# Hybrid conformer and MLA block: new durations and a longer assumed landing time in the kernel's own scheduler

## Chip, cores, metric

One core of one Trainium2 chip. The metric is the device time of one execution in microseconds; the median of several runs counts. The profile is one more execution, taken by the hardware profiler.

## What is computed

One decoder block on x (512 tokens of width 1024, float32). Six vectors of width 1024 (shift, scale and gate for the mixer and for the MLP) come from the conditioning vector c by one product with w_ada; they modulate the normalised x. Cut to what matters:

```python
mod = silu(c) @ w_ada + b_ada                      # 1024 -> 6 * 1024
shift1, scale1, gate1, shift2, scale2, gate2 = split(mod, 6)
h = rms_norm(x, g_pre_mix) * (1 + scale1) + shift1
u_glu, q_lat, kv_lat, k_r, gate_logits = split(h @ w_in)
u = causal_depthwise_conv(ua * sigmoid(ub), conv_w, conv_b)      # 31 taps, 1024 channels
y_a = silu(layer_norm(u, conv_norm_g, conv_norm_b)) @ w_conv_out
o = mla_attention(q_nope, q_rope, k_nope, k_rope, v)             # 8 heads, causal
y_b = o @ w_attn_out
y = (sigmoid(g_a) * y_a + sigmoid(g_b) * y_b) @ w_out
x = x + gate1 * rms_norm(y, g_post_mix)
h = rms_norm(x, g_pre_mlp) * (1 + scale2) + shift2
x = x + gate2 * rms_norm(square(relu(h @ w_mlp_in)) @ w_mlp_out, g_post_mlp)
```

## The kernel before

Each float32 product is made of three products of a rounded form: an operand is split into a high half (a cast by ScalarE, ACT) and a low half (a subtraction by VectorE, DVE), and `mm3` (line 454) issues high x high, high x low and low x high on TensorE (PE). Weights are loaded by SyncE (SP) in units of 512 KB or so, split, used and dropped (`wunit`, line 492). All buffers lie in two large tiles, `f_arena` (float32) and `r_arena` (the split halves), and in the eight banks of `psum`; an allocator gives out places, and an instruction that writes a place waits until whoever read it before has finished.

**The stages in the order of PE's work:** the first input products, with shift1 and scale1 made just in time (to about 70 us); the rest of the input projection; attention by heads (from about 150 to 275 us): `proj` (line 1008) makes q and k of a head, and `v_pair` (984) makes V for two heads; `scores` (1032) makes four tiles of scores and a softmax; `pv` (1057) transposes the probabilities on PE, splits them into halves and multiplies by V. For the last two heads V is kept in float32 and copied by ACT out of psum. Then the products with w_attn_out, the gates, a LayerNorm, w_conv_out, w_out, and from about 510 us the MLP in four chunks.

**Work beside it.** The depthwise convolution is 31 multiply-adds for each of eight channel tiles, all on DVE with the weights in the tile `cw` (`conv_ops`, line 783; 240 scalar_tensor_tensor and 8 tensor_scalar in all). They depend on nothing but each other and may stand anywhere until the LayerNorm. The modulation rows for gate1, shift2 and scale2 are made in attention by `ada_by_dma` (1134): SP loads 1 MB of w_ada (two blocks of 1024 columns by 128 partitions); ACT multiplies each block by the matching column of c (`act.mul`, operand `cT`); GpSimd (POOL) issues a DMA which adds the block to one of three sums in `f_arena`. That is 12 loads, 24 multiplications and 21 adding transfers. Transfers into the same sum follow one another, each waiting for the last to land. The loaded buffer comes free only when its adding transfers have landed.

**What sets the order.** Nothing runs in the order of the code. Every call goes to `Planner.record` (245), which stores it with its cost (`cost`, 217) and the calls it depends on. `Planner.plan` (306) then plays the program through: at each moment each engine takes, of the calls whose inputs are ready, PE the earliest in the code, and every other engine the one that is due first (a few calls have a bonus); due times are worked back from PE's sequence. A DMA is held to occupy a common channel for its bytes and to land 910 ns after it. The calls are then issued in the order of their starts (line 388, the line of nearly all instructions in the profile). So each engine gets a fixed queue. The whole is repeated up to eight times with buffers placed by the lifetimes of the time before, and the repetition with the shortest plan is kept.

Of the kernel before, what the change touches and what calls it, by code (L numbers as in the profile page):

```python
# [45 lines left out]
PV32 = (3,)  # L46
PASSES = 8
LEAD = 15000.0
ADAS = (1, 1, 0, 4)
KGRP = ((2, 3), (4, 5), (6,), (7,))  # L50
HX, HA, HG, HC = 1.2e5, 1e5, 3e3, 1.1e5
# [109 lines left out]


class Op:
    __slots__ = ("i", "eng", "fn", "a", "k", "cost", "post", "deps", "succ", "dead", "t0", "t1", "ndep", "ready", "dma", "rank", "hurry", "bufs", "raw")


class Planner:
# [6 lines left out]
    def __init__(self, nc, spaces):  # L174
        self.spaces = spaces
        self.real = dict(pe=nc.tensor, act=nc.scalar, dve=nc.vector, pool=nc.gpsimd, sp=nc.sync)
        self.ops = []
        self.last_w = {}
        self.reads = {}
        self.boost = 0  # L180
        self.hurry = 0.0
        self.after = None

    class Engine:
        def __init__(self, plan, name):
# [31 lines left out]
    def cost(self, eng, fn, outs, ins, k):  # L217

        n = max(self.free_size(o) for o in (ins if fn == "reduce_sum" else outs))
        if fn == "dma_start":  # L220
            return 475.0, 2000.0
        psum = any(r.tensor.name.startswith("psum") for r in ins + outs)
        if eng == "pe":
            if fn == "transpose":
                return 0.85 * n + 1, 190.0
            if ins[0].dtype == F32:
                return max(53.5, n / 2.4 + 2) * 4, 190.0
            return max(64.0, n / 2.4 + 2.5), 190.0
        scalars = sum(isinstance(v, bass.AP) and self.free_size(v) == 1 for v in ins) if n > 1 else 0
        if eng == "act":  # L230
            t = 0.833 * n + (51 if psum else 93) + 93 * scalars
            if fn == "activation" and any(isinstance(v, bass.AP) for v in outs[1:]):
                t += 93
            return t, 150.0
        if eng == "dve":
            if fn in ("tensor_copy", "tensor_scalar"):
                return (1.04 if psum else 0.52) * n + 68 + 61 * scalars, 150.0
            if fn == "scalar_tensor_tensor":
                return 1.04 * n + 130, 150.0
            return 1.04 * n + 70, 150.0  # L240
        if fn == "memset":
            return 36.0, 100.0
        return (460.0 if ALU.pow in self.args else 160.0) + 1.0 * n, 150.0

    def record(self, eng, fn, a, k):
        self.args = a
        aps = [v for v in a if isinstance(v, bass.AP)]
        names = dict(k)
        outs, ins = [], []
        if "out" in names:  # L250
            outs.append(names.pop("out"))
        else:
            outs.append(aps.pop(0))
        if fn == "tensor_tensor_reduce":
            outs.append(aps.pop())
        if isinstance(names.get("accum_out"), bass.AP):
            outs.append(names.pop("accum_out"))
        ins = aps + [v for v in names.values() if isinstance(v, bass.AP)]
        o = Op()
        o.i, o.eng, o.fn, o.a, o.k = len(self.ops), eng, fn, a, k  # L260
        o.succ, o.dma, o.rank, o.hurry = [], None, len(self.ops) - self.boost, self.hurry
        o.cost, o.post = self.cost(eng, fn, outs, ins, k)
        if fn == "dma_start":
            b = 4
            for _, c in outs[0].ap:
                b *= c
            o.dma = b
        deps = set()
        rd = [self.region(r) for r in ins]
        wr = [self.region(w) for w in outs]  # L270
        o.bufs = set()
        for nm, units in rd + wr:
            for sp in self.spaces:
                if nm.startswith(sp):
                    o.bufs.add((sp, self.spaces[sp].owner[units[0]]))
        for nm, units in rd:
            lw, rs = self.last_w.setdefault(nm, {}), self.reads.setdefault(nm, {})
            for u in units:
                if u in lw:
                    deps.add(lw[u])  # L280
        o.raw = set(deps)
        for nm, units in wr:
            lw, rs = self.last_w.setdefault(nm, {}), self.reads.setdefault(nm, {})
            for u in units:
                if u in lw:
                    deps.add(lw[u])
                if u in rs:
                    deps.update(rs[u])
        for nm, units in rd:
            rs = self.reads[nm]  # L290
            for u in units:
                rs.setdefault(u, []).append(o.i)
        for nm, units in wr:
            lw, rs = self.last_w[nm], self.reads[nm]
            for u in units:
                lw[u] = o.i
                rs.pop(u, None)
        deps.discard(o.i)
        if self.after is not None:
            deps.add(self.after)  # L300
        o.deps = deps
        for d in deps:
            self.ops[d].succ.append(o.i)
        self.ops.append(o)

    def plan(self):
        ops = self.ops
        pe_t = 0.0
        big = sum(o.cost for o in ops if o.eng == "pe") + TAIL
        for o in ops:  # L310
            o.dead = big
            if o.eng == "pe":
                pe_t += o.cost
                o.dead = pe_t
        for o in reversed(ops):
            lat = o.post + (o.dma / 180.0 if o.dma else 0.0)
            for s in o.succ:
                q = ops[s]
                o.dead = min(o.dead, q.dead - q.cost - lat)
        heaps = {e: [] for e in self.NAMES}  # L320
        free = {e: 0.0 for e in self.NAMES}
        dma_free = 0.0
        future = []

        def key(o):
            return (o.rank, o.i) if o.eng == "pe" else (o.dead - o.hurry, o.i)

        for o in ops:
            o.ndep, o.ready = len(o.deps), 0.0
            if not o.ndep:  # L330
                heapq.heappush(future, (0.0, o.i))
        order = []
        now = 0.0
        while len(order) < len(ops):
            while future and future[0][0] <= now:
                o = ops[heapq.heappop(future)[1]]
                heapq.heappush(heaps[o.eng], (key(o), o.i))
            for e in self.NAMES:
                if free[e] <= now and heaps[e]:
                    o = ops[heapq.heappop(heaps[e])[1]]  # L340
                    o.t0 = now
                    free[e] = now + o.cost
                    if o.dma:
                        st = max(now + 1100.0, dma_free)
                        dma_free = st + o.dma / 360.0
                        o.t1 = dma_free + 910.0
                    else:
                        o.t1 = free[e] + o.post
                    order.append(o)
                    for s in o.succ:  # L350
                        q = ops[s]
                        q.ndep -= 1
                        q.ready = max(q.ready, o.t1 if (q.eng != o.eng or o.dma) else free[e] if e == "pe" else max(free[e], o.t1 - 30))
                        if not q.ndep:
                            heapq.heappush(future, (q.ready, q.i))
            nxt = [free[e] for e in self.NAMES if free[e] > now and heaps[e]]
            if future:
                nxt.append(future[0][0])
            if not nxt:
                break  # L360
            now = max(now, min(nxt)) if min(nxt) > now else now
        assert len(order) == len(ops)
        self.length = max(o.t1 for o in ops)
        return order
# [28 lines left out]
def tile_hybrid_block(  # L393
# [48 lines left out]
    def emit(past, replay):  # L442
# [3 lines left out]
        plan = Planner(nc, dict(f_arena=fa, r_arena=ra, psum=pb))  # L446
        pe, act, dve, pool, sp = (plan.engine(e) for e in Planner.NAMES)
# [52 lines left out]
        st = tile_of([P, 96], F32, "stats")  # L500
# [43 lines left out]
        for t in range(NT):  # L544
            b = fa.alloc(D)
# [7 lines left out]
        for i, vecs in enumerate(((("bada", b_ada), ("gpm", g_pre_mix)),  # L553
# [5 lines left out]
            for nm, src in vecs:  # L559
                n = src.shape[1] // P  # L560
# [50 lines left out]
        for k in range(KD):  # L611
            b = pb.alloc()
# [77 lines left out]
        for ks in KGRP:  # L690
            plan.hurry = HA - 1e4 * ks[0]
            n = len(ks) * P
# [441 lines left out]
        def ada_by_dma(parts):  # L1134
# [3 lines left out]
                ada_acc[part] = fa.alloc(D)  # L1138
            for u in range(4):
                for part in parts:  # L1140
                    acc = fa.v(ada_acc[part])
                    b = fa.alloc(2 * D)
                    v = fa.v(b, "p (j n) -> p j n", j=2)
                    sp.dma_start(out=v, in_=w_ada[u * 256:(u + 1) * 256, part * D:(part + 1) * D].rearrange("(j p) n -> p j n", p=P))
                    for jj in range(2):
# [3 lines left out]
                        else:  # L1149
                            act.mul(v[:, jj], v[:, jj], cT[:, j:j + 1])  # L1150
                            pool.dma_start(out=acc, in_=v[:, jj], accum_op=ALU.add)
                    fa.free(b)
                    yield

        late = ada_by_dma((2, 3, 4))
# [204 lines left out]
        for t in range(NT):  # L1360
            b = fa.alloc(D)
# [290 lines left out]
```

## Time and profile before

| | before |
|---|---|
| median of 3 runs (lowest to highest) | 848.84 us (845.19 to 849.06) |
| profiled execution, time | 851.26 us |
| profiled execution, span | 849.5 us |
| PE busy | 812.4 us (96%) |
| DVE busy | 660.6 us (78%) |
| ACT busy | 444.5 us (52%) |
| POOL busy | 45.9 us (5%) |
| mean granted TensorE clock | 0.985 |
| DMA | 128.28 MB, 151 GB/s in the mean |

The span runs from the first to the last instruction of that one execution; its own time holds a little more around it. Busy time counts instructions at work; for PE the ends are modelled, so short waits can hide in it. Where a row has a bracket like [7.12 <-ACT r_arena L388], the engine was idle for so many us before it, and the wait was ended by that engine's instruction writing that tile. SPq and POOLq are the queues that issue DMAs.

### The profile page before, as it was taken

The page shows a single profiled execution, that of the slowest core. Times are in us where ns is not written, and L with a number is a line of the kernel's source. Part 1 is how long each engine was busy: PE and PEld are TensorE (multiplying, and loading weights), DVE is VectorE, ACT ScalarE, POOL GpSimd, SP SyncE. Part 2 cuts the span into 40 slices and gives each one's busy share as a digit, 9 for nine tenths or more (in the row PEclk, how much of TensorE's full clock was granted, in tenths as well). Part 3 has the DMA queues.
Part 4 walks back from the last instruction along what each step waited for, and adds up shares of the span by engine and source line. Part 5 has one row for each costly group of instructions (what it writes and reads, how often), then busy time and mean ns, then how long its engine had stood idle before and what let it go on. Part 6 is the DMA issues. An engine that isn't in the chain of part 4 may idle for free.

```text
span 849.5 us, 10707 instructions
## 1 busy us (share of the span) xinstructions
PE 812.4 (96%) x3940; PEld 678.0 (80%) x3940; DVE 660.6 (78%) x988; ACT 444.5 (52%) x736; POOL 45.9 (5%) x105
## 2 busy tenths in 40 slices
PE   6989999887979999999999999999999999999995
PEld 3767988776978888888888879888888888888884
DVE  3979989776869999998966278478629993986596
ACT  5463374567669536325824268466346443643552
POOL 2001020111110000001000020000000000000001
PEclk9999999997989999999999999999999999999998
DMA  9997424877879834013586034037004850570202
GB/s 308 326 307 232 143 74 131 204 200 197 227 212 277 243 76 123 26 50 100 174 276 218 26 137 137 25 110 237 1 26 124 269 176 27 176 244 1 100 0 100
DMA packets 89846, 128.28 MB, mean 151 GB/s; under 512 B 7610, under 2 KB 60963, under 8 KB 89794
## 3 DMA queue, kind: packets, MB, share of 16 engines
q1 hardware_dynamic: 86770, 116.59, 43.0%
q0 software_dynamic: 3024, 11.01, 7.1%
q8 instruction: 31, 0.51, 0.2%
q14 instruction: 21, 0.17, 0.1%
HBM read 108.18 MB, written 8.39 MB: 137 GB/s over the span
## 4 chain that ended last, share of the span: by engine, by line
PE 81%; DMA 10%; DVE 3%; ACT 3%; issue 1%; POOL 1%; SPq 0%; POOLq 0%; DVEq 0%; ACTq 0%
PE psum L388 81%; DMA f_arena<-in_w_ada_dram 3%; DVE f_arena L388 3%; DMA f_arena<-in_w_in_dram 2%; DMA f_arena<-f_arena 2%; ACT f_arena L388 2%; DMA f_arena<-in_w_ukv_dram 1%; ACT r_arena L388 1%; DMA f_arena<-in_w_uq_dram 1%; DMA c<-in_c_dram 1%; POOL stats L388 1%; DVE r_arena L388 1%; SPq L388 0%; ACT stats L388 0%; POOLq L1647 0%
## 5 line engine op out<-in xcount | busy, mean ns | idle before, releaser
L388 PE MATMUL psum<-r_arena 128*128 128x512 f32 (+2 forms) x3592 | 770.4, 376 | 15.2 <-ACT r_arena L388 14.2
L388 PEld LDWEIGHTS psum<-r_arena 128*128 128x128 f32 x3592 | 636.6, 191 | 133.3 <-ACT r_arena L388 16.1
L388 DVE TENSOR_TENSOR r_arena<-f_arena,r_arena 128x1024 fp32r<-128x1024 f32 (+4 forms) x232 | 248.3, 1093 | 104.8 <-PE psum L388 53.8
L388 ACT CAST r_arena<-f_arena 128x1024 fp32r<-128x1024 f32 (+4 forms) x222 | 209.3, 965 | 181.2 <-PE psum L388 105.5
L388 DVE SCALAR_TENSOR_TENSOR f_arena<-f_arena,cw 128x512 f32<-128x512 f32 x240 | 165.2, 750 | 0.3
L388 ACT ACTIVATE f_arena<-psum 128x512 f32<-128x512 f32 x64 | 37.9, 596 | 118.6 <-PE psum L388 118.6
L388 DVE TENSOR_TENSOR f_arena<-f_arena 128x1024 f32<-128x1024 f32 (+3 forms) x78 | 77.3, 1006 | 6.3 <-ACT f_arena L388 3.6
L388 ACT ACTIVATE f_arena<-f_arena 128x512 f32<-128x512 f32 (+3 forms) x100 | 58.3, 605 | 12.9 <-DVE f_arena L388 11.6
L388 DVE TENSOR_TENSOR f_arena<-psum,f_arena 128x512 f32<-128x512 f32 x52 | 35.3, 686 | 20.2 <-PE psum L388 20.1
L388 DVE TENSOR_TENSOR r_arena<-psum,r_arena 128x512 fp32r<-128x512 f32 (+2 forms) x57 | 35.9, 657 | 16.2 <-ACT r_arena L388 15.8
L388 PE MATMUL psum<-ident,f_arena 128*128 128x128 f32 (+1 forms) x240 | 35.5, 287 | 11.9 <-DVE f_arena L388 11.4
L388 PEld LDWEIGHTS psum<-ident,f_arena 128*128 128x128 f32 (+1 forms) x240 | 28.8, 147 | 18.2 <-DVE f_arena L388 13.3
L388 POOL TENSOR_TENSOR stats<-stats,nhalf 128x1 f32<-128x1 f32 x24 | 16.7, 706 | 481.4 <-ACT stats L388 481.4
L388 ACT ACTIVATE f_arena<-f_arena,cT 128x1024 f32<-128x1024 f32 x24 | 27.4, 1155 | 21.6 <-DMA f_arena<-in_w_ada_dram 19.6
L388 ACT CAST r_arena<-psum 128x512 fp32r<-128x512 f32 (+2 forms) x57 | 30.0, 563 | 7.4 <-PE psum L388 7.1
L388 ACT COPY f_arena<-psum 128x512 f32<-128x512 f32 (+4 forms) x42 | 19.8, 499 | 21.9 <-PE psum L388 21.5
L388 DVE SCALAR_TENSOR_TENSOR f_arena<-f_arena,cT 128x256 f32<-128x256 f32 (+2 forms) x63 | 28.5, 510 | 0.1
L388 POOL DMA_DIRECT2D f_arena<-f_arena x21 | 18.5, 911 | 150.7 <-ACT f_arena L388 105.8
L388 ACT ACTIVATE r_arena<-f_arena 128x512 fp32r<-128x512 f32 (+3 forms) x20 | 12.9, 648 | 18.8 <-DVE f_arena L388 16.2
L388 DVE CUSTOM_DVE_ANT_0 f_arena<-psum,mask 128x128 f32<-128x128 f32 (+3 forms) x32 | 14.9, 486 | 3.3 <-PE psum L388 3.2
L388 DVE TENSOR_SCALAR f_arena<-f_arena,stats 128x1024 f32<-128x1024 f32 x8 | 6.0, 751 | 10.6 <-POOL stats L388 10.6
L388 DVE SCALAR_TENSOR_TENSOR f_arena<-f_arena 128x512 f32<-128x512 f32 (+1 forms) x18 | 13.3, 747 | 0.0
(96 smaller groups left out, 204.2 us busy)
## 6 DMA issues: line engine op xcount, KB each, us to landing
f_arena<-in_w_ada_dram SPq DMA_DIRECT2D x16, 1024.0 KB, 6.3
f_arena<-in_w_mlp_in_dram SPq DMA_DIRECT2D x32, 512.0 KB, 4.2
f_arena<-in_w_mlp_out_dram SPq DMA_DIRECT2D x32, 512.0 KB, 5.6
f_arena<-in_w_in_dram SPq DMA_DIRECT2D x28, 512.0 KB, 8.5
f_arena<-f_arena POOLq DMA_DIRECT2D x21, 512.0 KB, 6.0
f_arena<-in_x_dram SPq DMA_DIRECT2D x8, 512.0 KB, 4.4
f_arena<-in_w_ada_dram SPq DMA_DIRECT2D x16, 256.0 KB, 5.7
f_arena<-in_w_ada_dram SPq DMA_DIRECT2D x8, 512.0 KB, 6.5
```

Source lines behind the costliest of these rows:

```text
L388: getattr(self.real[o.eng], o.fn)(*o.a, **o.k)
```

## The change

The planner's numbers change, and nothing that is computed. A DMA issue is held to cost 850 ns on POOL and 375 on the other engines (475 on all before). A matmul in the split form is held to cost at least 109 ns and otherwise n / 2.4 + 13.3 (64 and n / 2.4 + 2.5 before). A POOL transfer counts 1.7 times its bytes, the channel moves 320 bytes a ns in place of 360, and both kinds of transfers in `ada_by_dma`, the loads and the adding ones, are held to land 8000 ns later than others. Due times use neither the channel's speed nor the 8000 ns.

```diff
+SLOW = 8000.0
...
         if fn == "dma_start":
-            return 475.0, 2000.0
+            return 850.0 if eng == "pool" else 375.0, 2000.0
...
-            return max(64.0, n / 2.4 + 2.5), 190.0
+            return max(109.0, n / 2.4 + 13.3), 190.0
...
+        o.slack = self.slack
         if fn == "dma_start":
             b = 4
             for _, c in outs[0].ap:
                 b *= c
-            o.dma = b
+            o.dma = b * 1.7 if eng == "pool" else b
...
-                        dma_free = st + o.dma / 360.0
-                        o.t1 = dma_free + 910.0
+                        dma_free = st + o.dma / 320.0
+                        o.t1 = dma_free + 910.0 + o.slack
...
             for u in range(4):
                 for part in parts:
+                    plan.slack = SLOW
                     acc = fa.v(ada_acc[part])
...
                     fa.free(b)
+                    plan.slack = 0.0
                     yield
```

With other numbers the play-through gives other queues and other places in the arenas. Three places show it. In the rows, `ISA f_arena<-psum,mask` is the masked maximum of a tile of scores and `ISA f_arena 128x1` the reading of its result, RECIPROCAL the inverse of a softmax sum, `cw` marks a product of the convolution, and `r_arena<-psum,r_arena` is the low half of a split.

DVE in late attention, before:

```order
262 L388 ISA f_arena 128x1
263 L388 RECIPROCAL f_arena<-f_arena 128x1
264 L388 SCALAR_TENSOR_TENSOR f_arena<-f_arena,cw 128x512
265 L388 ISA f_arena<-psum,mask 128x512
266 L388 ISA f_arena 128x1
267 L388 RECIPROCAL f_arena<-f_arena 128x1
268 L388 SCALAR_TENSOR_TENSOR f_arena<-f_arena,cw 128x512
269 L388 TENSOR_TENSOR r_arena<-psum,r_arena 128x512 x2
270 L388 TENSOR_TENSOR r_arena<-psum,r_arena 128x256
271 L388 RECIPROCAL f_arena<-f_arena 128x1 x2
272 L388 SCALAR_TENSOR_TENSOR f_arena<-f_arena,cw 128x512 x3
273 L388 TENSOR_TENSOR r_arena<-psum,r_arena 128x512 x2
```

DVE at the like place now, from the last softmax tiles of a head to the split of its transposed probabilities:

```order
299 L391 ISA f_arena<-psum,mask 128x128
300 L391 ISA f_arena 128x1
301 L391 RECIPROCAL f_arena<-f_arena 128x1
302 L391 SCALAR_TENSOR_TENSOR f_arena<-f_arena,cw 128x512 x2
303 L391 RECIPROCAL f_arena<-f_arena 128x1
304 L391 SCALAR_TENSOR_TENSOR f_arena<-f_arena,cw 128x512 x38
305 L391 TENSOR_SCALAR f_arena<-f_arena,cw,cols_103 128x512
306 L391 SCALAR_TENSOR_TENSOR f_arena<-f_arena,cw 128x512 x8
307 L391 TENSOR_SCALAR f_arena<-f_arena,cw,cols_103 128x512
308 L391 SCALAR_TENSOR_TENSOR f_arena<-f_arena,cw 128x512 x15
309 L391 TENSOR_TENSOR r_arena<-psum,r_arena 128x512
310 L391 ISA f_arena<-psum,mask 128x384
```

Before, one to three products stand between two softmax or split instructions; now 38 + 1 + 8 + 1 + 15 = 63 stand in a row ahead of the split in row 309.

PE in late attention, before, with what each row waits for: a head's probabilities are transposed (`ident`), and the products with V (row 317 and on) stand among scores:

```order
306 L388 MATMUL psum<-ident,f_arena 128x128 [waits Activation_49] x2
307 L388 MATMUL psum<-ident,f_arena 128x128 [waits DVE_49]
308 L388 MATMUL psum<-ident,f_arena 128x128 [waits Activation_49]
309 L388 MATMUL psum<-ident,f_arena 128x128
310 L388 MATMUL psum<-ident,f_arena 128x128 [waits DVE_49]
311 L388 MATMUL psum<-ident,f_arena 128x128 [waits Activation_49]
312 L388 MATMUL psum<-ident,f_arena 128x128 x3
313 L388 MATMUL psum<-r_arena 128x128 [waits DVE_49,Activation_49]
314 L388 MATMUL psum<-r_arena 128x128 [waits DVE_49]
315 L388 MATMUL psum<-r_arena 128x128 x3
316 L388 MATMUL psum<-r_arena 128x256 x4
317 L388 MATMUL psum<-r_arena 128x512 [waits Activation_49]
```

PE now, at the place that belongs to the DVE rows above: scores to row 322, the transposes of the probabilities, the scores of the next head, whose bank ACT must first copy out (row 325), and the products with V from row 330:

```order
322 L391 MATMUL psum<-r_arena 128x384 x4
323 L391 MATMUL psum<-ident,f_arena 128x128 [waits Activation_49] x3
324 L391 MATMUL psum<-ident,f_arena 128x128 x2
325 L391 MATMUL psum<-r_arena 128x512 [waits Activation_49]
326 L391 MATMUL psum<-r_arena 128x512 x2
327 L391 MATMUL psum<-r_arena 128x384 [waits Activation_49]
328 L391 MATMUL psum<-r_arena 128x384 x4
329 L391 MATMUL psum<-r_arena 128x512 x2
330 L391 MATMUL psum<-r_arena 128x512 [waits Activation_49]
331 L391 MATMUL psum<-r_arena 128x512 [waits DVE_49]
332 L391 MATMUL psum<-r_arena 128x512
333 L391 MATMUL psum<-r_arena 128x384 x3
```

Row 325 waits for ACT's copy of V, and that copy for an adding transfer, since V has been given a place that a modulation buffer held. Row 330 waits for the cast of the probabilities, row 331 for their low half on DVE, row 309 above.

SP from the first half of attention on, before: loads of w_ada stand between the small loads of w_uq and w_ukv:

```order
68 L388 DMA f_arena<-in_w_ada_dram 128x2x1024
69 L388 DMA f_arena<-in_w_uq_dram 128x2x128 x3
70 L388 DMA f_arena<-in_w_ada_dram 128x2x1024 x2
71 L388 DMA f_arena<-in_w_uq_dram 128x4x64 x3
72 L388 DMA f_arena<-in_w_ada_dram 128x2x1024 x2
73 L388 DMA f_arena<-in_w_uq_dram 128x2x128 x2
74 L388 DMA f_arena<-in_w_ada_dram 128x2x1024
75 L388 DMA f_arena<-in_w_uq_dram 128x2x128
76 L388 DMA f_arena<-in_w_ada_dram 128x2x1024
77 L388 DMA f_arena<-in_w_attn_out_dram 128x4x256
```

SP now:

```order
68 L391 DMA f_arena<-in_w_ukv_dram 128x2x512
69 L391 DMA f_arena<-in_w_uq_dram 128x2x128 x3
70 L391 DMA f_arena<-in_w_uq_dram 128x4x64 x3
71 L391 DMA f_arena<-in_w_ada_dram 128x2x1024 x3
72 L391 DMA f_arena<-in_w_ukv_dram 128x2x512
73 L391 DMA r_arena<-h_spill_68 128x512
74 L391 DMA f_arena<-in_w_ada_dram 128x2x1024 x2
75 L391 DMA f_arena<-in_w_attn_out_dram 128x4x256
76 L391 DMA f_arena<-in_w_uq_dram 128x2x128 x3
77 L391 DMA f_arena<-in_w_ukv_dram 128x2x512
78 L391 DMA f_arena<-in_w_ada_dram 128x2x1024
```

The w_uq loads for the second rotary half (128x4x64) now stand ahead of a group of three w_ada loads; before they stood behind four of them. ACT's queue changes alike: now four modulation multiplications stand together ahead of the two copies of V:

```order
202 L391 ACTIVATE f_arena<-f_arena 128x384
203 L391 ACTIVATE f_arena<-f_arena 128x128
204 L391 ACTIVATE f_arena<-f_arena,cT 128x1024 x4
205 L391 COPY f_arena<-psum 128x512 x2
206 L391 CAST r_arena<-psum 128x512
207 L391 CAST r_arena<-f_arena 128x1024
```

Before, one stands two copies ahead of the next:

```order
183 L388 ACTIVATE f_arena<-f_arena 128x512
184 L388 COPY f_arena<-psum 128x512
185 L388 CAST r_arena<-psum 128x512
186 L388 COPY f_arena<-psum 128x512
187 L388 ACTIVATE f_arena<-f_arena 128x128
188 L388 ACTIVATE f_arena<-f_arena,cT 128x1024
189 L388 ACTIVATE f_arena<-f_arena 128x256
```

More of the change, by code (lines that the diff above doesn't have):

```diff
@@ L163 @@
 class Op:
-    __slots__ = ("i", "eng", "fn", "a", "k", "cost", "post", "deps", "succ", "dead", "t0", "t1", "ndep", "ready", "dma", "rank", "hurry", "bufs", "raw")
+    __slots__ = ("i", "eng", "fn", "a", "k", "cost", "post", "deps", "succ", "dead", "t0", "t1", "ndep", "ready", "dma", "rank", "hurry", "bufs", "raw", "slack")
 class Planner:
@@ L182, in __init__ @@
         self.after = None
+        self.slack = 0.0
     class Engine:
```

## The prediction

> **What bounds the kernel now.** I read the page's first lines, then TensorE's timeline, then a table by stretch, and last the waits.
>
> ```profile
> span 849.5 us, 10707 instructions
> PE 812.4 (96%) x3940; PEld 678.0 (80%) x3940; DVE 660.6 (78%) x988; ACT 444.5 (52%) x736; POOL 45.9 (5%) x105
> ...
> 600.00:700.00 100.00, 100.00 (x443) 82.84 (x442) 71.88 (x70) 47.27 (x57) 0.00 (x0) 1.00 0.39 126
> ```
>
> TensorE (PE) is the bound. In the MLP 443 matmuls of 512 columns fill 100 us, 0.226 us each, and nothing there can be gained by another order. What an order can win or lose is the time in which PE waits. Outside the start and the tail, TensorE's timeline has these waits of more than a quarter of a microsecond in the attention stage, from 160 to 260 us:
>
> ```profile
> 165.65 0.66 PE L388 MATMUL psum<-ident,f_arena 128*128 128x128 f32 x4 [2.97 <-DVE f_arena L388]
> 185.41 0.55 PE L388 MATMUL psum<-ident,f_arena 128*128 128x128 f32 x3 [0.28 <-DVE r_arena L388]
> 186.87 0.77 PE L388 MATMUL psum<-ident,f_arena 128*128 128x128 f32 x5 [0.92 <-DVE f_arena L388]
> 195.92 10.45 PE L388 MATMUL psum<-r_arena 128*128 128x512 f32 x42 [7.12 <-ACT r_arena L388]
> 240.22 13.81 PE L388 MATMUL psum<-r_arena 128*128 128x512 f32 x68 [4.33 <-ACT r_arena L388]
> ```
>
> They sum to 15.6 us. A wait costs more than itself, as the table by stretch shows (its last three columns are the granted clock, the DMA share and GB/s):
>
> ```profile
> 190.00:200.00 10.00, 4.08 (x10) 3.31 (x11) 4.69 (x10) 5.49 (x12) 1.77 (x2) 0.59 0.69 191
> 200.00:210.00 10.00, 10.00 (x57) 9.08 (x56) 6.73 (x20) 7.64 (x19) 0.87 (x1) 0.90 0.83 205
> ...
> 230.00:240.00 10.00, 5.89 (x38) 4.98 (x36) 5.96 (x14) 5.23 (x13) 0.19 (x1) 0.98 0.82 227
> 240.00:250.00 10.00, 9.78 (x43) 8.70 (x44) 7.32 (x17) 7.46 (x17) 0.87 (x1) 0.68 0.92 287
> ```
>
> If the clock is either full or half, 0.59 is 8.2 us of half clock and 0.90 is 2.0 us. In the first stretch PE works only 4.1 us, after its wait; so about 6.1 us of work ran at half speed and lost 3.05 us. The same sum over the second pair gives 6.4 us at half, 3.1 us lost. Waits and clock together: 15.6 + 6.2 = 21.8 us.
>
> Who causes the waits? The chain that ended last runs through them:
>
> ```profile
> 181.68 5.11 DMA f_arena<-f_arena
> ...
> 186.83 6.73 DMA f_arena<-in_w_ada_dram
> ...
> 193.65 1.75 ACT f_arena L388 x3
> 195.40 0.48 ACT r_arena L388
> ...
> 195.92 5.93 PE psum L388 x17
> ```
>
> An adding transfer lands, only then may SyncE (SP) issue the next load of modulation weights, ScalarE (ACT) stands before the multiplication that needs that load, and behind it in ACT's queue stands the cast that PE waits for. Over the whole run (waiting engine, what it waited for, total, times, longest):
>
> ```profile
> SPq L388 <- DMA f_arena<-f_arena: 73.2, 12, 16.4
> ACT f_arena L388 <- DMA f_arena<-in_w_ada_dram: 19.6, 6, 5.5
> ...
> f_arena<-in_w_ada_dram SPq DMA_DIRECT2D x16, 1024.0 KB, 6.3
> f_arena<-f_arena POOLq DMA_DIRECT2D x21, 512.0 KB, 6.0
> ```
>
> **The change part by part.** No instruction is added or removed; new numbers in the planner reorder every queue and move buffers.
>
> *The adding transfers and their loads.* The order now allows for late landings. On SP the w_uq loads of the second rotary half stood behind four modulation loads and now stand ahead of all; the last w_ukv load stood behind ten and now stands behind five. With landings assumed 8 us later than the planner would otherwise take them, the measured 6.0 and 6.3 us are on time. I therefore take all 21.8 us as gone. Bounds: if half of the waits only move, 11; if all stay, 0.
>
> *A run of convolution products on VectorE (DVE).* This is the step that decides. DVE's new order has, between the last reciprocal of one head's softmax and the subtraction that makes the low half of that head's transposed probabilities, 61 scalar_tensor_tensor products with cw and 2 tensor_scalar (rows 304 to 308, 38 + 1 + 8 + 1 + 15). PE's rows 330 and 331 wait for the cast and then for that very subtraction (row 309). Before, at most three products stand between two such instructions there. The planner fills a wait that it foresees for the transfers; but the queue is fixed, so the products stay in front however early the transfers land. The rows that price it:
>
> ```profile
> L388 DVE SCALAR_TENSOR_TENSOR f_arena<-f_arena,cw 128x512 f32<-128x512 f32 x240 | 165.2, 750 | 0.3
> ...
> 232.06 0.29 DVE L388 CUSTOM_DVE_ANT_0 f_arena<-psum,mask 128x128 f32<-128x128 f32 x1
> ...
> 253.22 0.55 DVE L388 CUSTOM_DVE_ANT_0 f_arena<-psum,mask 128x384 f32<-128x384 f32 x1
> 253.70 0.08 DVE L388 DVE_READ_ACCUMULATOR2_ANT f_arena<- 128x1 f32 x1
> 253.70 0.16 DVE L388 RECIPROCAL f_arena<-f_arena 128x1 f32<-128x1 f32 x1
> ...
> 275.22 1.00 DVE L388 TENSOR_SCALAR f_arena<-f_arena,cw,cols 128x512 f32<-128x512 f32 x2
> ...
> 280.45 0.69 DVE L388 TENSOR_TENSOR r_arena<-psum,r_arena 128x512 fp32r<-128x512 f32 x1
> ...
> 282.82 5.39 DVE L388 SCALAR_TENSOR_TENSOR f_arena<-f_arena,cw 128x512 f32<-128x512 f32 x8
> ```
>
> Products that follow each other take 5.39 / 8 = 0.67 us; the group's 165.2 / 240 = 0.69 is the upper price. The run: 61 x 0.67 + 2 x 0.50 = 41.9 us. It cannot begin early, because its first instruction stands behind a reciprocal that needs the maximum and sum of score tiles which PE has just made (row 322 on PE, 128x384). From PE's last score matmul to the run DVE has 0.55 + 0.08 for that tile, 0.29 + 0.08 for the next, three reciprocals of 0.16 and three products of 0.67: 3.5 us. Behind the run comes the subtraction, 0.69. In sum 3.5 + 41.9 + 0.7 = 46.1 us from the end of row 322 to the start of row 331.
>
> PE has little to do meanwhile: rows 323 and 324 are 5 transposes, rows 325 to 330 are 11 matmuls.
>
> ```profile
> 129.57 2.78 PE L388 MATMUL psum<-ident,f_arena 128*128 128x128 f32 x24
> ```
>
> 5 x 2.78 / 24 = 0.6 us and at most 11 x 0.226 = 2.5 us. So PE idles 46.1 - 3.1 = 43.0 us. After so long a wait it starts at half clock; from the row at 195.92 that loses 3.05 us. Term: +46.0 us. Bounds: 61 x 0.69 and 2 us more for reciprocals that wait for ACT give 49; products at 0.66 and no clock loss give 42.
>
> The Trainium skill's page "TensorE: Matmul & The Clock Gate" (section "What's actually happening") gives about 3.4 us of sustained work until the full clock is back, where the stretches here show 6.1. By that figure a restart would lose some 1.7 us (an estimate from that page), that is the two old ones 2.7 us less than I remove and the new one 1.35 us less than I add; the sum would stand 1.4 us higher. The measurement decides.
>
> *The same place, transfers alone.* PE's row 325 waits for ACT's copies of V in row 205, which stand behind four modulation multiplications (row 204) and go into a buffer that an adding transfer reads. In series there: an adding transfer 6.0, a load 6.3, a multiplication, an adding transfer 6.0, a copy.
>
> ```profile
> L388 ACT ACTIVATE f_arena<-f_arena,cT 128x1024 f32<-128x1024 f32 x24 | 27.4, 1155 | 21.6 <-DMA f_arena<-in_w_ada_dram 19.6
> ```
>
> That is 6.0 + 6.3 + 1.2 + 6.0 + 0.6 = 20.1 us (0.6 is my estimate for a 512-column copy, half the multiplication's 1.155), of which about 5 lie beside PE's work before the end of row 322 (an estimate: some 25 short matmuls stand between the first transfer's issue and that row): some 15 us of waiting, wholly inside the 46. It costs nothing while the DVE run stands; it would be late next if the run were not there.
>
> *Start, mixer's end, tail.* Small loads move ahead of modulation loads at the start, x and w_out loads interleave at the end of the mixer, and DVE has 63 products fewer later, where PE does not wait for them. Between -3 and +6 us, the latter for small waits of PE for a ScalarE that has more multiplications close together in late attention; I take +2.
>
> Sum against the profiled execution: 849.5 - 21.8 + 46.0 + 2 = 875.7 us of span. That execution took 851.26 us, 1.8 more than its span, so 877.5; the median of the runs is 848.84, a factor of 0.997 below it: **875 us**.
>
> **The rivals.**
>
> *Faster: the run is hidden (chance 0.05).* If the products were done before PE makes those scores, or if DVE could take the subtraction ahead of them, the old waits would be gone and nothing new come: 849.5 - 21.8 + 2 = 829.7, a median of 829. It decides once no more than about 5 products (PE's own 3.1 us) stand between reciprocal and subtraction. For it speaks that the transfers land earlier than the planner believes; against it, that the run stands in DVE's fixed order and its head depends on PE. The skill's page "Perfetto Trace Analysis" (section "Tensor Engine Instruction") calls DVE a strict FIFO; by that rule this case cannot come from overtaking.
>
> *No change: the transfers set the wait, not DVE (0.05).* If the subtraction's place mattered less than I read, the 15 us with 3 of clock would stand against the 21.8: 849.5 - 21.8 + 18 + 2 = 847.7, a median of 847.
>
> *The change does not do what it says (0.08).* SP and ACT go on standing before late transfers elsewhere in attention, so that nothing of the 21.8 goes, and the run comes on top: 849.5 + 46 = 895.5, a median of 895. For it: 73.2 us of SP's waiting is much to remove by an order. Against it: the assumed landing exceeds the measured one.
>
> **How the numbers follow.** The forecast has 0.82. Its own range takes the run's bounds (42 to 49), the old waits (11 to 21.8 removed) and the last term (-3 to +6): 866 at the low end with the run at 42 and -3; 890 at the high end, where the run is at 49, a part of the old waits stays and small ones come. The spread of the runs shown (845.19 to 849.06) takes 2 more off the low end: 864 to 890, which leaves out the two cheap rivals and the dearest. A measurement of this kernel can tell about 0.5% from no change, here 4.2 us: faster has the first rival's 0.05, the same the second's 0.05, slower the other 0.90.
>
> **What would show it.** In the profile after: on TensorE's timeline between 215 and 300 us a wait of about 27 us for DVE behind one of about 15 for ACT, with eleven matmuls between; on DVE at that place a run of some 42 us of products with cw and no pause; mean granted clock near 0.97, lower than before. SP's wait for adding transfers well under 73 us, and no wait of PE over 2 us between 160 and 215 us, would show the first step right. If PE's long wait is some 15 us and DVE's products lie elsewhere, the second rival holds; if waits near 7 and 4 us are still there before it, the third. With no wait over 10 us at all, the forecast is wrong in its main step.

## The result, and the profile after

| | before | after |
|---|---|---|
| median (lowest to highest), 4 runs each | 848.33 us (845.19 to 849.06) | 886.02 us (883.41 to 889.41) |
| profiled execution, time | 851.26 us | 885.15 us |
| its span | 849.5 us | 883.3 us |
| mean granted TensorE clock | 0.985 | 0.966 |

The kernel after is slower: ratio 1.0454, 95% interval 1.0408 to 1.0500. The forecast was 875 us in a range of 864 to 890.

The page after, its first lines and the rows of PE and of the granted clock in 40 slices of 22 us:

```profile
span 883.3 us, 10710 instructions
PE 817.0 (92%) x3940; PEld 678.4 (77%) x3940; DVE 660.9 (75%) x988; ACT 446.2 (51%) x736; POOL 52.3 (6%) x105
PE   6899999899951499999999999999999999999996
...
PEclk9989999999985599999999999999999999999998
```

Every engine has the work it had (PE 812.4 us before, DVE 660.6). Each digit is the busy share of a slice in tenths, and in the second row the granted clock in tenths. The loss is a hole in PE's row in the twelfth to fourteenth slice, and the clock falls in the same place. TensorE's timeline from 252 to 305 us:

```profile
252.73 0.98 PE L391 MATMUL psum<-r_arena 128*128 128x256 f32 x5
255.82 0.33 PE L391 MATMUL psum<-ident,f_arena 128*128 128x128 f32 x1 [2.10 <-ACT f_arena L391]
256.71 0.33 PE L391 MATMUL psum<-ident,f_arena 128*128 128x128 f32 x1 [0.56 <-ACT f_arena L391]
257.50 0.90 PE L391 MATMUL psum<-ident,f_arena 128*128 128x128 f32 x3 [0.47 <-ACT f_arena L391]
277.75 4.03 PE L391 MATMUL psum<-r_arena 128*128 128x512 f32 x11 [19.34 <-ACT f_arena L391]
298.99 5.60 PE L391 MATMUL psum<-r_arena 128*128 128x512 f32 x16 [17.22 <-DVE r_arena L391]
```

Five transposes, a wait of 19.34 us for ACT, eleven matmuls, a wait of 17.22 us for DVE. The timeline of all engines shows what both do meanwhile (`cw` marks a convolution product, `cT` a modulation multiplication, COPY a copy of V, SPq the queue that issues loads):

```profile
256.93 25.25 DVE L391 SCALAR_TENSOR_TENSOR f_arena<-f_arena,cw 128x512 f32<-128x512 f32 x38
...
258.84 16.20 SPq L391 DMA_DIRECT2D f_arena<-in_w_ada_dram  x3
...
269.54 2.19 ACT L391 ACTIVATE f_arena<-f_arena,cT 128x1024 f32<-128x1024 f32 x2 [12.09 <-DMA f_arena<-in_w_ada_dram]
...
274.00 2.19 ACT L391 ACTIVATE f_arena<-f_arena,cT 128x1024 f32<-128x1024 f32 x2 [2.28 <-DMA f_arena<-in_w_ada_dram]
...
277.11 1.07 ACT L391 COPY f_arena<-psum 128x512 f32<-128x512 f32 x2 [0.92 <-DMA f_arena<-f_arena]
...
282.55 5.39 DVE L391 SCALAR_TENSOR_TENSOR f_arena<-f_arena,cw 128x512 f32<-128x512 f32 x8
...
288.30 10.03 DVE L391 SCALAR_TENSOR_TENSOR f_arena<-f_arena,cw 128x512 f32<-128x512 f32 x15
298.24 0.70 DVE L391 TENSOR_TENSOR r_arena<-psum,r_arena 128x512 fp32r<-128x512 f32 x1
```

Two chains end here. DVE works without a pause from 256.93 to 298.24 us, 38, 8 and 15 products and two tensor_scalar, before the subtraction that PE's 298.99 waits for. Meanwhile ACT goes through loads, four multiplications and an adding transfer before the copies that PE's 277.75 waits for. The chain that ended last takes the first of the two:

```profile
251.54 1.94 DVE f_arena L391 x6
254.09 42.99 DVE f_arena L391 x73
298.99 7.03 PE psum L391 x27
```

SyncE's waits for adding transfers are 31.5 us (73.2 before):

```profile
SPq L391 <- DMA f_arena<-f_arena: 31.5, 4, 12.3
```

### The profile page after: what moved, and what is told of

It is laid out like the page before. It is cut to its first block, busy times and chain, and to the rows that moved or that the text cites. A ratio compares the mean times of both kernels' runs of the same rounds, so it can differ in the third digit from the quotient of the medians.

```text
span 883.3 us, 10710 instructions
## 1 busy us (share of the span) xinstructions
PE 817.0 (92%) x3940; PEld 678.4 (77%) x3940; DVE 660.9 (75%) x988; ACT 446.2 (51%) x736; POOL 52.3 (6%) x105
## 4 chain that ended last, share of the span: by engine, by line
PE 72%; DVE 20%; ACT 3%; DMA 2%; issue 1%; POOL 1%; DVEq 0%; SPq 0%; ACTq 0%
PE psum L391 72%; DVE f_arena L391 15%; DVE r_arena L391 5%; DMA f_arena<-in_w_in_dram 2%; ACT r_arena L391 2%; ACT f_arena L391 1%; POOL stats L391 0%; DMA f_arena<-in_x_dram 0%; ACT stats L391 0%; POOL lns L391 0%; DVE lns L391 0%; DVEq L1652 0%; SPq L391 0%; DVE mod L391 0%; DVEq L391 0%
## 5 line engine op out<-in xcount | busy, mean ns | idle before, releaser
L391 PE MATMUL psum<-r_arena 128*128 128x512 f32 (+3 forms) x3592 | 772.7, 375 | 38.8 <-ACT f_arena L391 19.3
L391 ACT ACTIVATE f_arena<-f_arena 128x512 f32<-128x512 f32 (+4 forms) x100 | 59.0, 607 | 36.9 <-DVE f_arena L391 35.8
L391 POOL TENSOR_TENSOR stats<-stats,nhalf 128x1 f32<-128x1 f32 x24 | 24.8, 1035 | 482.6 <-ACT stats L391 482.4
L391 PE MATMUL psum<-ident,f_arena 128*128 128x128 f32 (+1 forms) x240 | 37.4, 296 | 15.5 <-DVE f_arena L391 11.4
L391 DVE TENSOR_TENSOR f_arena<-psum,f_arena 128x512 f32<-128x512 f32 x52 | 35.1, 689 | 15.7 <-PE psum L391 15.6
L391 ACT CAST r_arena<-psum 128x512 fp32r<-128x512 f32 (+2 forms) x57 | 30.3, 565 | 10.1 <-PE psum L391 9.8
L391 ACT COPY f_arena<-psum 128x512 f32<-128x512 f32 (+4 forms) x42 | 19.5, 495 | 16.5 <-PE psum L391 15.6
L391 DVE SCALAR_TENSOR_TENSOR f_arena<-f_arena,psum 128x512 f32<-128x512 f32 x16 | 11.0, 686 | 7.6 <-PE psum L391 6.0
```

What stands on the lines that cost most here:

```text
L391: getattr(self.real[o.eng], o.fn)(*o.a, **o.k)
```

## The experiments

My theory: DVE's run sets the loss, the transfers end 20 us earlier in its shadow and would be late next, and the run is there because the planner fills a gap that the assumed landings open. The main rival: the transfers set both waits. Ratios are against runs of the kernel before on the same chip; its medians are 846.38 us beside the first four kernels, 849.91 beside the next four and 849.39 beside the last four. Single times compared across these groups are good to some 3 us.

### Two chains at one place: leave out one, the other, both

**Without the run's products** (found in the order as DVE's longest stretch that reads cw):

```diff
+        run, best = [], []
...
+        best = {i for i in best if self.ops[i].fn == "scalar_tensor_tensor"}
         for o in order:
+            if o.i in best:
+                continue
```

> The kernel after, with the 61 scalar_tensor_tensor products of the run on DVE left out (the convolution loses these taps); order, buffers and all else stay. My theory: two chains end at the same place, DVE's run (PE's wait of 17.2 us behind the eleven matmuls) and the modulation's transfers (PE's wait of 19.3 us for ACT's copies). Without the run only the second wait is left: 886 less 17.2 and less one restart at half clock (1.7 to 3) gives 866 to 867 us, and the wait for ACT stays at 19.3. Rival, the transfers alone set both waits: 886, nothing changes. Rival, the run alone sets both: 840.

Measured: 867.08 us (864.08 to 867.81), ratio 1.0234 (1.0204 to 1.0264). PE's timeline at the place:

```profile
259.16 0.90 PE L402 MATMUL psum<-ident,f_arena 128*128 128x128 f32 x3 [0.47 <-ACT f_arena L402]
279.74 6.80 PE L402 MATMUL psum<-r_arena 128*128 128x512 f32 x27 [19.67 <-ACT f_arena L402]
```

The 27 matmuls that stood in two pieces run in one, and the wait for ACT is left as it was.

**Without the adding transfers:**

```diff
         for o in order:
+            if "accum_op" in o.k:
+                continue
```

> The kernel after, with its 21 adding transfers left out when it is issued (three modulation rows keep only their first terms); order, buffers, loads and multiplications stay. My theory: the run on DVE ends when it did, so the time stays within 2 us of 886; PE's wait for ACT becomes short and its wait for DVE longer by as much, together about 36 us. Rival, the transfers alone set both waits: the time falls to about 850.

Measured: 883.97 us (883.37 to 884.76), ratio 1.0441 (1.0415 to 1.0467); its span is 883.0, against 883.3. PE's timeline, with one row of DVE:

```profile
257.89 25.25 DVE L393 SCALAR_TENSOR_TENSOR f_arena<-f_arena,cw 128x512 f32<-128x512 f32 x38
...
267.53 4.52 PE L393 MATMUL psum<-r_arena 128*128 128x512 f32 x11 [8.16 <-ACT f_arena L393]
...
299.94 5.59 PE L393 MATMUL psum<-r_arena 128*128 128x512 f32 x16 [27.89 <-DVE r_arena L393]
```

The wait moved from ACT to DVE: 8.16 + 27.89 = 36.05, where it was 19.34 + 17.22 = 36.56. The rival falls.

**Without both** (the two edits together):

> The kernel after, with both left out: the 61 products of the run and the 21 adding transfers. My theory of two chains that hide each other: both waits go, down to at most 9 us for loads of modulation weights, 842 to 853 us. Then the 61 products alone are worth 17 to 20, the transfers alone nothing, both together 33 to 44. Rival, one of the two alone is the cause: this time equals that of the kernel in which that one is left out.

Measured: 854.92 us (853.57 to 855.95), ratio 1.0096 (1.0070 to 1.0123). At the place one wait is left, for loads alone:

```profile
267.86 7.41 PE L404 MATMUL psum<-r_arena 128*128 128x512 f32 x27 [8.16 <-ACT f_arena L404]
```

So from 886.0 us: the products alone are worth 18.9, the transfers alone 2.0 (not to be told from nothing), both 31.1; by the ratios, which stay within one group of runs for each kernel, 18.6, 1.1 and 30.3. That is neither a sum nor one cause: each chain hides the other. It is 2 us above what I expected; the 8.16 was at the end of my "at most 9", and small waits that I had not counted stay too.

**The kernel before without its adding transfers** (the same edit):

> The kernel before, with its 21 adding transfers left out and all else the same. My first term took 21.8 us for the waits for late transfers in attention: 848.3 less 21.8 is 826.5; PE's waits of 7.1 and 4.3 us are gone. Rival, the loads of modulation weights are late by themselves, whatever the adding transfers do: at least half of the waits stays, 837 or more.

Measured: 827.76 us (825.90 to 828.19), ratio 0.9778 (0.9750 to 0.9806). From 10 to 560 us TensorE's timeline has three waits of half a microsecond or more:

```profile
60.84 0.50 PE L390 MATMUL psum<-r_arena 128*128 128x512 f32 x1 [0.62 <-ACT r_arena L390]
62.28 4.83 PE L390 MATMUL psum<-r_arena 128*128 128x512 f32 x20 [0.93 <-DVE r_arena L390]
...
483.68 1.08 PE L390 MATMUL psum<-r_arena 128*128 128x256 f32 x4 [1.60 <-ACT r_arena L390]
```

That is 18.6 us less than the kernel before beside it, 20.6 less than the 848.33 of the result: the 21.8 us of the first term are the adding transfers' price to within some 3 us. It also shows that the two chains are not all: the kernel after with both of them out (854.92) still takes 27 us more than this one. Its waits of half a microsecond or more between 10 and 560 us sum to 20.8 us where this one has 3.2: 8.16 for the loads, 5.1 in the start, 3.0 near 170 us and smaller ones; half clock behind some of them comes on top.

### What makes the planner leave the gap

Each of these plans the whole program anew; nothing is left out of the work. **The new durations without slack** (`SLOW = 0.0`):

> The kernel after with SLOW = 0, so the new durations alone without the longer landing. The longest run of convolution products on DVE is 17 there, not 63. My theory, that the 8 us of assumed landing make the planner foresee the wait that it fills with products: no run, but the old late transfers are back, so 850 to 862 us (before's waits, and up to 6 us at the start and in attention that the new durations cost), with PE waits of 3 to 7 us for ACT between 180 and 260. Rival, the new durations alone make the gap: 875 or more.

Measured: 838.85 us (836.77 to 839.46), ratio 0.9888 (0.9828 to 0.9949): about 1% less than before, where I had expected the old waits back and 850 to 862. The longest wait of PE from 160 to 280 us is this one:

```profile
189.27 8.17 PE L391 MATMUL psum<-r_arena 128*128 128x512 f32 x44 [0.72 <-ACT r_arena L391]
```

My theory of the old waits falls here: the slack is not needed to get rid of the late transfers, the new durations do it too.

**The slack without the new durations** (before, with SLOW = 8000 on the same calls):

> The kernel before with SLOW = 8000 alone: the longer landing with the old durations. The longest run of products is 17. My theory: the waits for late transfers go (my first term, 21.8) and no gap comes, 826 to 833 us, about as without the adding transfers. Rival, 8 us of landing make the gap whatever the durations: 870 or more.

Measured: 833.23 us (832.51 to 833.89), ratio 0.9820 (0.9769 to 0.9870), 0.2 above my range. No gap either; one wait in attention's tail is new:

```profile
314.37 1.97 PE L391 MATMUL psum<-ident,f_arena 128*128 128x128 f32 x8 [3.13 <-ACT f_arena L391]
```

**New durations, slack of 3 us** (`SLOW = 3000.0`):

> The kernel after with SLOW = 3000 and all else as it is. The longest run of products is 13. My theory: the landing is still long enough for the measured one and too short to make the gap, so run and waits are both gone: 830 to 842 us, the start up to 5 us worse than before. Rival, part of the landing brings part of the loss of 37: 860 to 875.

Measured: 841.17 us (839.64 to 843.63), ratio 0.9905 (0.9878 to 0.9932). No run and no late transfer, but a wait in the start and one near 169 us:

```profile
44.84 0.61 PE L391 MATMUL psum<-ones,f_arena 128*128 128x1 f32 x4 [3.04 <-DVE f_arena L391]
...
169.05 1.12 PE L391 MATMUL psum<-ident,f_arena 128*128 128x128 f32 x4 [3.01 <-DVE f_arena L391]
```

**Old durations, slack of 4 us:**

> The kernel before with SLOW = 4000 and the old durations. The longest run of products is 17. Theory: as with 8000, no wait of PE over 2 us for a transfer in attention, 824 to 832 us, the fastest of these four with the old start. Rival, 4 us are too little and the wait of 7 us near 190 stays: 837 or more.

Measured: 828.39 us (824.95 to 830.40), ratio 0.9758 (0.9700 to 0.9817). This one beats both kernels, and gains as much as the kernel before does without its adding transfers (0.9778). Two rows of its table by stretch, where before PE worked 4.08 and 5.89 us of ten (after the length come the busy times of PE, of its weight loads, of DVE, ACT and POOL):

```profile
190.00:200.00 10.00, 10.00 (x61) 8.88 (x59) 9.31 (x24) 9.64 (x22) 0.93 (x2) 1.00 0.88 193
...
230.00:240.00 10.00, 10.00 (x63) 9.04 (x62) 9.00 (x22) 9.34 (x20) 1.74 (x2) 1.00 0.60 137
```

Then one duration at a time. **After, with the old duration of a matmul:**

```diff
-            return max(109.0, n / 2.4 + 13.3), 190.0
+            return max(64.0, n / 2.4 + 2.5), 190.0
```

> The kernel after with the old duration of a matmul, max(64, n/2.4 + 2.5), and all else as it is (SLOW 8000 too). DVE's order has a run of 69 products at the same place. Theory: the run decides, so 880 to 893 us, with PE waiting for ACT and DVE there together some 36 to 46 us; if the matmul's duration is what costs the start its 5 us, PE's waits at 44 and 49 us are gone. Rival, the longer matmul is what makes the gap: 850 or less.

Measured: 893.67 us (892.91 to 896.57), ratio 1.0564 (1.0518 to 1.0609), 0.7 above the range. The run and both waits are there, a little longer:

```profile
44.43 0.60 PE L391 MATMUL psum<-ones,f_arena 128*128 128x1 f32 x4 [2.25 <-DVE f_arena L391]
...
276.75 4.10 PE L391 MATMUL psum<-r_arena 128*128 128x384 f32 x10 [20.99 <-ACT f_arena L391]
299.64 5.60 PE L391 MATMUL psum<-r_arena 128*128 128x512 f32 x16 [18.79 <-DVE f_arena L391]
```

The matmul's duration does not make the gap. Nor does it cost the start: the wait at 44 us stays.

**After, with the old channel:**

```diff
-                        dma_free = st + o.dma / 320.0
+                        dma_free = st + o.dma / 360.0
```

> The kernel after with the old channel of 360 bytes per ns in place of 320 and all else as it is (SLOW 8000 too). The longest run of products is 19, near 105 us. Theory: the gap is a tipping of the plan, where slack and a slower channel add up; without one of them no run and no late transfer, 832 to 846 us. Rival, 8 us of landing with recorded matmuls make the waits for transfers by themselves, run or not: 855 to 870.

Measured: 846.72 us (844.54 to 848.29), ratio 0.9978 (0.9958 to 0.9999). The gap is gone with 8 us of slack kept. It is 0.7 above my range. There is a wait in the start that I had not foreseen, beside smaller ones near 170 (2.05 us) and 323 us (3.57):

```profile
48.15 1.01 PE L391 MATMUL psum<-ones,f_arena 128*128 128x1 f32 x4 [7.71 <-DVE f_arena L391]
```

**Before, with the new duration of a matmul alone:**

> The kernel before with the new duration of a matmul alone (no slack, old channel, old transfer costs). Theory, after the kernel without slack came out without the old waits: a later believed landing removed them there, not the matmul's duration, so here the waits of 7 and 4 us stay: 844 to 856 us. Rival, the matmul's duration removed them: 835 to 841.

Measured: 852.89 us (850.39 to 855.63), ratio 1.0062 (1.0034 to 1.0090). The late transfers are still there:

```profile
199.64 10.22 PE L391 MATMUL psum<-r_arena 128*128 128x512 f32 x41 [5.43 <-ACT r_arena L391]
```

**Before, with the channel of 320 alone:**

> The kernel before with the channel of 320 bytes per ns alone (no slack, old durations else). Theory: a later believed landing of every transfer removes most of the old waits, 830 to 841 us. Rival, only what is said of the adding transfers themselves helps (slack or their bytes): 844 to 852.

Measured: 838.65 us (838.36 to 839.28), ratio 0.9907 (0.9876 to 0.9937). Most of the old waits are gone; 3.18 us are left of the 7.12:

```profile
187.47 9.69 PE L391 MATMUL psum<-r_arena 128*128 128x512 f32 x44 [3.18 <-ACT r_arena L391]
```

What follows: a landing that the planner believes to be later removes the late transfers, wholly or for the greater part, whichever number makes it later (slack of 4 or 8, or the slower channel). The gap comes where the slack of 8 and the slow channel are together: with 3 us of slack or none it does not open, nor with the old channel. The two were not tried without the new issue costs and the factor of 1.7 on POOL's bytes, so that they suffice by themselves is not shown. The kernels with 3 us of slack and with the old channel do all the products too (841.17 and 846.72 us), which speaks for the place of the products, and not their number, as what costs. That the planner takes the products because its due times know of neither number is argued from the code, not shown by a run.

## Why the prediction was right, point by point

**The main step held.** I put 46.1 us between the end of PE's row 322 and the start of row 331. Row 322 ends at 252.73 + 0.98 = 253.71 and row 331 starts at 298.99: 45.3 us. The run took 41.3 us from 256.93 to 298.24, against 41.9. PE's own 3.1 us taken off, 42.2 are lost (43.0 forecast), and the restart behind it costs half of 5.95 us at half clock, 3.0 (3.05 forecast). The term is 45.2 where I had 46.0. That the restart cost what the one at 195.92 had cost is in part luck: the restart at 277.75, after 19.34 us of waiting, ran 3.30 us at half clock and cost 1.65. The rows of the clock (stretch, its length, PE's busy time and in brackets its instructions, the granted clock, where 0.50 is half, the DMA share and GB/s):

```profile
257.16:281.05 23.89, 4.21 (x12) 0.50 1.02 286
281.05:284.46 3.41, 0.72 (x3) 1.00 1.03 203
284.46:304.94 20.48, 5.95 (x19) 0.50 0.16 30
304.94:308.35 3.41, 3.36 (x19) 1.00 0.64 196
```

**The transfers inside it** I sized at 15 us of waiting, and they are 19.3. What I said of them held: they cost nothing while the run stands (883.97 us without them) and are late next once it is gone (867.08 with a wait of 19.67). For that reason the run, though it set the end, was worth only 18.9 us when it was left out: the second chain ended some 20 us before the first, and set the time from there on.

**The old waits: 21.8 removed, in fact 17.1.** This is a term mis-sized. The waits of 7.12 and 4.33 us are gone, as are the two small ones. But the wait of 2.97 us near 165 us is there again, 3.03, with 3.41 us at half clock behind it (1.7 lost):

```profile
168.41:171.82 3.41, 3.41 (x13) 2.92 (x13) 3.41 (x7) 2.65 (x3) 1.34 (x2) 0.50 0.93 317
```

It is not the same wait. In the kernel before it goes when the adding transfers go; in the kernel after it stays without them (3.01 us). With the old duration of a matmul it is absent from the kernel after. What is late there is DVE, which works without a pause from 160 to 170 us with convolution products among its own steps; that these products make it late is read from the trace and was not tried. DVE's busy time is the third pair; after, then before:

```profile
160.00:170.00 10.00, 6.97 (x42) 6.12 (x41) 10.00 (x19) 1.62 (x3) 0.49 (x2) 0.92 0.70 179
```

```profile
160.00:170.00 10.00, 7.03 (x47) 6.23 (x46) 5.63 (x11) 5.66 (x9) 1.72 (x2) 1.00 0.76 146
```

I took a wait as gone since its transfer would be on time, and did not ask what else the new order puts ahead of the same matmul. That is the question that I did ask at row 309.

**Start and rest: +2, in fact +5.0.** PE in the first 80 us, before and then after (columns as in the rows of the clock):

```profile
0.00:80.00 80.00, 70.23 (x321) 1.00 0.95 298
```

```profile
0.00:80.00 80.00, 68.64 (x301) 0.96 0.91 285
```

PE is idle for 11.36 us in place of 9.77, 1.6 more. It also works through two stretches of half clock, where the kernel before has full clock, and these lose half of 6.8 us, 3.4:

```profile
45.53:48.94 3.41, 3.41 (x9) 0.50 0.93 262
...
52.36:55.77 3.41, 3.41 (x11) 0.50 1.06 362
```

Together that is 5.0 us. The waits ahead of them:

```profile
44.27 0.60 PE L391 MATMUL psum<-ones,f_arena 128*128 128x1 f32 x4 [2.82 <-DVE f_arena L391]
...
51.16 3.64 PE L391 MATMUL psum<-r_arena 128*128 128x512 f32 x10 [1.23 <-ACT r_arena L391]
```

It is within the -3 to +6 that I gave. Which number causes it stays open: such waits come with the slower channel alone (1.21 and 1.23 us) and with the old channel beside all the rest (7.71), but not with slack alone or the matmul alone.

**The sum.** 849.5 - 17.1 + 45.2 + 5.0 = 882.6 against 883.3 measured; 0.7 us I have not placed. The median lies 2.7 above the profiled span here, where I took it 0.7 below, as before's runs had it. So the 11.0 us between 875 and 886 are 4.7 from the old waits, 3.0 from the start, 0.7 unplaced and 3.4 from median against span, less 0.8 from the run. All but the last go the same way. My bounds, all at their dear end, add up to about 893 (849.5 - 11 + 49 + 6, less 0.7 for the median), where I put 890; 886.0 lies below both.

**The rivals.** "The run is hidden" (829) falls: it stood in front to the end. "The transfers set the wait" (847) falls by the second experiment. "The change does not do what it says" (895) falls in the main, with 3.0 of 15.6 us back for another reason. My reason for the first term was wrong in part: I gave the credit to the 8 us alone, and the durations without them reach 838.85 us.

**What would show it.** An ACT wait of about 15 and a DVE wait of about 27 with eleven matmuls between: 19.3 and 17.2, with eleven between. The sum was near and the split was not: the wait for ACT was 4.3 longer, 3.1 us of waiting stood already before the transposes, and PE's few instructions, at half clock, took longer than I had counted (4.03 us for the eleven, where I had 2.5); all this comes off the wait for DVE. A run of 42 us: 41.3. Clock near 0.97: 0.966. SyncE's wait well under 73: 31.5. No PE wait over 2 us between 160 and 215: wrong, 3.03.

## What to carry to other kernels

When a scheduler is told that a transfer is late, look for what it puts into the gap in each engine's fixed queue: here 42 us of harmless products that no early landing could move out of the way. Two corrections that each gain (838.9 and 833.2 us, beside 849.9) can lose together (886.0, beside 848.3), so a planner's numbers have to be tried together as well as one by one, and in small steps (4 us of slack with the old durations gave 828.4, the best that does the whole work). Where two chains end at one place, taking one away shows only the distance to the other; take both away before you put a price on either.

## What the runs showed of the hardware

The granted clock changes in steps of one length. After the two waits it stands at half for 23.89 and 20.48 us, 7 and 6 times 3.41; the row at 168.41 is one such step. So what a restart loses depends on where in a step the work begins: at 277.75 us PE ran 3.30 us at half clock, at 298.99 us 5.95 us, after waits of nearly the same length. The Trainium skill's page "TensorE: Matmul & The Clock Gate" (section "What's actually happening") describes a free-running window of about 3.4 us. These rows agree, and with them both the 3.4 and the 6.1 of the prediction have their place: the longer figure is the rest of a window that had begun while PE was idle (304.94 less two windows is 298.11, and PE began at 298.99), and then a whole one.

A wait of some 3 us can cost a step or not. The one of 3.03 us that ended at 168.41 did; the one of 2.97 us in the kernel before did not, where the clock is 1.00 from 160 to 170 us.

The products on DVE did not notice the adding transfers: 38 of them took 25.25 us with the transfers beside them, when DMA moved 282 GB/s, and 25.25 us without, at 130 GB/s.
